# Gated-recurrence trunk on one core: the first heads' pk in a free buffer, lb behind the last values, and the 64-row level beside the block product

## The chip, the core and the metric

One core of one Trainium2 chip runs the whole program. The metric is device microseconds (us) for one execution, the median of several runs. Each run's time lies a little above the span that its profile shows, which counts from the first to the last instruction.

## The reference

Two layers, each on 256 rows of 1024 columns (float32):

```
h = rmsnorm(x); proj = h @ w_in            # split into hq hf hi hg aq ak av ga gb
f  = lb + (1-lb)*sigmoid(hf); k = 1-f; q = silu(hq); v = hi     # 8 heads of 128
S_t = f_t * S_(t-1) + k_t v_t^T ;  o_t = q_t S_t                # gated linear recurrence
y_a = (rmsnorm_per_head(o) * silu(hg)) @ w_pa
y_b = sliding_window_attention(aq, ak, av, sinks) @ w_pb        # 16 query, 4 key heads of 64
x  += (sigmoid(ga)*y_a + sigmoid(gb)*y_b) @ w_o
x  += (silu(h2 @ w_gate) * (h2 @ w_up)) @ w_down                # h2 = rmsnorm(x)
```

and a last rmsnorm. The recurrence is written out as scores: score(t, s) is the sum over the 128 columns c of q(t,c) k(s,c) times the product of f(c) over the rows after s up to t.

## The kernel before

**The main stream.** All large products (the projections, yb, ya, wo, the feed-forward) are run by TensorE as matmuls of 128 x 128 by 512 columns. Every weight is split into a high and a low part (wh by ScalarE, wl by VectorE) ahead of its use, and each product takes three matmuls (wh by high, wl by high, wh by low). A generator of the main stream gives way after every 6 such matmuls; this is called a step here. In the order of the main stream a layer runs akv, aq, v, then pb (the forget gate and query of the recurrence), gate, gb and yb in halves, ga, ya, wo, and then the feed-forward. gate, gb, yb and ga have 48 matmuls in each half.

**Side work.** Attention, recurrence, norms and transposes are generators on a list; after each step of the main stream every one whose count of steps has run out is moved on. So the matmuls of side work stand between those of the main stream in groups, called visits here. The numbers that such a generator yields (`YB`, `YD`, `YQ`, `YN`, `GAPS`) are how many steps to let pass: they set where a visit stands. Instructions of the other engines are put in order by a scheduler, engine by engine; TensorE's in visits are kept as written. A helper records every operation, so that nearly all instructions of a trace have its line, L57, and go by the names of their tiles.

**Attention** (`attention`): for four groups n of heads, `attend` makes scores (qk), `turn` transposes the weights (pt; ScalarE copies them back into the tile sp), and `values` multiplies them with v (pv). The tile sp is one buffer with the tag "sp". After `turn(3)`, `YB` steps pass, and then the last two `values` run in one visit.

**Recurrence** (`recurrence`, `decays`, `chain`): heads go in two halves, g = 0 and g = 1, and each has a `chain`. `decays` makes f, q and k. The chain makes the scores within 128 rows level by level, from 4 rows up: pk (VectorE products of q with f) and lb for blocks of 4; p2 and lc for blocks of 16; lv for the levels of 16, 32 and 64 rows; each time VectorE multiplies f into q and k for the next level, and the scores are gathered in sd and st. lx is the block product between rows 0 to 127 and 128 to 255, o the product with v (sx is the copy of lx that it reads), ot the transpose of the normed result, which ya reads. One visit serves both halves, with g = 1 one phase behind: the visits of a layer are lb of g = 0 alone, then lb with lc, lc with lv of 16 rows, lv 16 with lv 32, lv 32 with lv 64, lv 64 with lx, lx with o, o with ot, and ot alone. lb and lc write 32 rows of the output at a time, as do lv of 16 and 32 rows (the trace's forms 128\*32); lv of 64 rows and pv write 64 (128\*64); lx, o, ot, pt and the main stream write all 128 (128\*128).

**What the change touches.** The tile pk of g = 0, and p2 after it, lie in the buffer of the tag "sp", which is attention's until its last `values` are done; those of g = 1 lie in the buffer "pk", which is free. `recurrence` waits until attention has ended (`while atd[0] is not None`) before it starts the chain of g = 0, whose first part makes pk. The lv of 64 rows multiplies q and k in place for lx after its matmuls were issued, so lx can only stand one visit later. Small tiles with the tag "hx" share four buffers.

## Time and profile before

| | |
|---|---|
| median of 3 runs | 936.68 us (935.9 to 936.97) |
| the profiled execution | 936.02 us, span 934.3 us |
| instructions | 14356 |
| TensorE matmul busy | 923.8 us, 99% of the span |
| VectorE busy | 674.9 us, 72% |
| ScalarE busy | 536.8 us, 57% |
| mean granted TensorE clock | 0.999 |

The table's busy times are of the whole span. An engine's idle time is listed with what ended it, and an instruction's row in order of time gives its start, its length, its engine, what it wrote and read, and its shape (contraction rows \* output rows, then the moving tile). A float32 product counts as two matmuls in a trace, one of the main stream as one. Matmul ends are modelled and overlap the next start, so for TensorE only the distances between starts are used.

### The profile page before, as it was taken

How to read it: one execution, taken by the hardware profiler on the slowest of the kernel's cores; microseconds unless marked ns; L12 is line 12 of the kernel's file. 1: busy time of each engine (PE TensorE's matmuls, PEld its weight loads, DVE VectorE, ACT ScalarE, POOL GpSimd, SP SyncE). 2: the span in 40 equal slices, each digit the busy share in tenths (PEclk: the TensorE clock that was granted, in tenths of full speed). 3: DMA queues.
4: the chain of work that ended last, by engine and by line, in shares of the span. 5: the costliest groups of instructions: out<-in, count | busy, mean ns of one | idle time of the engine just before them, and what ended most of it. 6: DMA issues, size and time to landing. Idle time of an engine off the chain costs nothing.

```text
span 934.3 us, 14356 instructions
## 1 busy us (share of the span) xinstructions
PE 923.8 (99%) x5716; PEld 779.7 (83%) x5716; DVE 674.9 (72%) x1169; ACT 536.8 (57%) x906; POOL 21.1 (2%) x33
## 2 busy tenths in 40 slices
PE   8999999999999999999999999999999999999997
PEld 6878888888888888888888888888888888888885
DVE  5667679974778767766756677799667787667665
ACT  5665795465546555554555767945454565455553
POOL 2000000001000000000000000000010000000000
PEclk9999999999999999999999999999999999999999
DMA  7846435554545665566477444545545465556641
GB/s 277 236 150 212 136 98 167 191 178 135 172 144 184 195 202 186 181 190 203 164 157 238 135 136 140 176 151 179 169 155 183 158 201 183 181 184 204 195 139 46
DMA packets 111459, 161.40 MB, mean 173 GB/s; under 512 B 2976, under 2 KB 64736, under 8 KB 111392
## 3 DMA queue, kind: packets, MB, share of 16 engines
q1 hardware_dynamic: 110608, 159.38, 53.3%
q8 instruction: 45, 0.74, 0.3%
q10 hardware_dynamic: 560, 0.84, 0.3%
q0 software_dynamic: 224, 0.26, 0.1%
q14 instruction: 22, 0.18, 0.1%
HBM read 159.42 MB, written 1.05 MB: 172 GB/s over the span
## 4 chain that ended last, share of the span: by engine, by line
PE 89%; ACT 5%; DVE 4%; issue 0%; POOL 0%; DVEq 0%; ACTq 0%; POOLq 0%
PE pg L57 13%; PE pu L57 13%; PE acc L57 13%; PE pb L57 7%; PE gb L57 5%; PE ga L57 5%; PE v L57 5%; PE yb L57 5%; PE wo L57 5%; PE ya L57 5%; PE aq L57 5%; PE akv L57 2%; DVE wl L57 2%; ACT sp L57 1%; ACT wh L57 1%; PE o L57 1%
## 5 line engine op out<-in xcount | busy, mean ns | idle before, releaser
L57 DVE TENSOR_TENSOR wl<-raw,wh 128x1024 fp32r<-128x1024 f32 (+1 forms) x301 | 364.5, 1219 | 136.7 <-ACT wh L57 135.5
L57 ACT CAST wh<-raw 128x1024 fp32r<-128x1024 f32 (+1 forms) x301 | 314.0, 1049 | 171.8 <-PE acc L57 47.7
L57 PE MATMUL pu<-xx_n,wh 128*128 128x512 f32 x352 | 92.6, 393 | 0.0
L57 PE MATMUL pg<-xx_n,wh 128*128 128x512 f32 x352 | 92.1, 393 | 0.0
L57 PEld LDWEIGHTS pg<-xx_n,wh 128*128 128x128 f32 x352 | 63.2, 189 | 11.0
L57 PEld LDWEIGHTS pu<-xx_n,wh 128*128 128x128 f32 x352 | 63.1, 189 | 10.9
L57 PE MATMUL acc<-wh,ah 128*128 128x512 f32 x174 | 68.2, 392 | 0.0
L57 PE MATMUL acc<-wh,al 128*128 128x512 f32 x174 | 67.8, 391 | 0.0
L57 PE MATMUL acc<-wl,ah 128*128 128x512 f32 x174 | 67.8, 390 | 0.0
L57 PE MATMUL pb<-xx_n,wh 128*128 128x512 f32 x256 | 66.3, 396 | 0.0
L57 PEld LDWEIGHTS pb<-xx_n,wh 128*128 128x128 f32 x256 | 45.4, 189 | 8.9 <-DVE wl L57 0.7
L57 PEld LDWEIGHTS pg<-xx_n,wl 128*128 128x128 f32 x352 | 48.4, 190 | 4.1 <-ACT xx_n L57 0.6
L57 PEld LDWEIGHTS pu<-xx_n,wl 128*128 128x128 f32 x352 | 48.4, 190 | 3.6
L57 PE MATMUL pg<-xx_n,wl 128*128 128x256 f32 x352 | 50.3, 284 | 0.0
L57 PE MATMUL pu<-xx_n,wl 128*128 128x256 f32 x352 | 49.8, 283 | 0.0
L57 ACT COPY zg<-pg 128x256 f32<-128x256 f32 x44 | 16.4, 372 | 53.4 <-PE pg L57 53.4
L57 PE MATMUL ga<-wh,xx_n 128*128 128x512 f32 x128 | 41.5, 396 | 0.0
L57 PE MATMUL gb<-wh,xx_n 128*128 128x512 f32 x128 | 41.2, 393 | 0.0
L57 ACT ACTIVATE sp<-sp,stat 128x128 f32<-128x128 f32 (+1 forms) x64 | 28.2, 442 | 22.5 <-DVE stat L57 22.5
L57 PE MATMUL gate<-wh,xx_n 128*128 128x512 f32 x128 | 41.0, 394 | 0.0
L57 PE MATMUL v<-wh,xx_n 128*128 128x512 f32 x128 | 41.0, 394 | 0.0
L57 PE MATMUL aq<-wh,xx_n 128*128 128x512 f32 x128 | 40.3, 391 | 0.0
(240 smaller groups left out, 1662.9 us busy)
## 6 DMA issues: line engine op xcount, KB each, us to landing
raw<-in_w_in SPq DMA_DIRECT2D x58, 1024.0 KB, 5.3
raw<-in_w_gate SPq DMA_DIRECT2D x22, 1024.0 KB, 5.0
raw<-in_w_up SPq DMA_DIRECT2D x22, 1024.0 KB, 5.1
raw<-in_w_down SPq DMA_DIRECT2D x22, 1024.0 KB, 5.0
raw<-in_w_pb SPq DMA_DIRECT2D x8, 1024.0 KB, 5.0
raw<-in_w_pa SPq DMA_DIRECT2D x8, 1024.0 KB, 5.1
raw<-in_w_o SPq DMA_DIRECT2D x8, 1024.0 KB, 4.9
raw<-in_w_in SPq DMA_DIRECT2D x3, 512.0 KB, 6.2
```

What stands on the lines that cost most here:

```text
L57: ins = call(*args, **kw)
```

## The change

Three things are edited, and the two tables of steps with them.

1. The tags of pk and p2 are exchanged: g = 0 takes the buffer "pk", g = 1 the buffer "sp".
2. The chain of g = 0 is started (its pk made) before `recurrence` waits for attention's end, and attention's generator ends right with its last `values` (no `yield 3` behind it). The lb of g = 0 is issued in the same pass of the side work, straight behind the pv of the last values. The last values themselves stand 5 steps behind `turn(3)` and not 3.
3. The level of 32 rows now also writes the operands of lx into two new tiles, qx and kx ("hx"): two halves are multiplied by VectorE into them (before: in place), two are copied by ScalarE. So lv of 64 rows and lx of the same half stand in one visit, and a chain has one phase less. `GAPS` has 8 entries and not 9.

```
-YB, YD, YQ = 3, 2, 5
+YD, YE, YQ = 2, 5, 5
-GAPS = ((8,), (6, 7), (3, 5), (3, 3), (2, 3), (1, 2), (3, 2), (4, 2), (1,))
+GAPS = ((8,), (6, 7), (3, 5), (4, 3), (3, 3), (4, 2), (4, 4), (1,))
...
             turn(3)
-            yield YB
+            yield YE
             together(values(2, "at"), values(3, "at"))
-            yield 3
...
-            pk = sm.tile([P, 32, 80], F32, tag=("sp", "pk")[g], name=f"pk{l}{g}", bufs=1)
+            pk = sm.tile([P, 32, 80], F32, tag=("pk", "sp")[g], name=f"pk{l}{g}", bufs=1)
...
-            p2 = sm.tile([P, 64, 24], F32, tag=("sp", "pk")[g], name=f"p2{l}{g}", bufs=1)
+            p2 = sm.tile([P, 64, 24], F32, tag=("pk", "sp")[g], name=f"p2{l}{g}", bufs=1)
...
-            m = 16
-            while m <= 64:
+            for m in (16, 32):
...
-                elif m == 64:
-                    A.copy(st[0:64, :, 64:128], ps[0:64])
...
-                    V.tensor_tensor(q4[:, :, 3], q4[:, :, 3], f4[:, :, 2, 0:1].to_broadcast([P, 4, m]), ALU.mult)
-                    V.tensor_tensor(k4[:, :, 0], k4[:, :, 0], f4[:, :, 1, 0:1].to_broadcast([P, 4, m]), ALU.mult)
...
+                    qx, kx = (ztile([P, 4, P], f"{n}x{l}{g}", "hx") for n in "qk")
...
+                    A.copy(qx[:, :, 0:64], q4[:, :, 2])
+                    A.copy(kx[:, :, 64:P], k4[:, :, 1])
+                    V.tensor_tensor(qx[:, :, 64:P], q4[:, :, 3], f4[:, :, 2, 0:1].to_broadcast([P, 4, 64]), ALU.mult)
+                    V.tensor_tensor(kx[:, :, 0:64], k4[:, :, 0], f4[:, :, 1, 0:1].to_broadcast([P, 4, 64]), ALU.mult)
                 yield
-            ps = psum(f"lx{l}{g}", tag).rearrange("p (i c) -> p i c", c=P)
+            ps = psum(f"lv{l}{g}64", tag).rearrange("p (i c) -> p i c", i=8)
+            for i in range(8):
+                h, a = i // 2, i % 2 * P
+                T.matmul(ps[0:64, i, :], k[:, h, a:a + 64], q[:, h, a + 64:a + P], start=True, stop=True)
+            px = psum(f"lx{l}{g}", tag).rearrange("p (i c) -> p i c", c=P)
             for h in range(4):
-                T.matmul(ps[:, h, :], k[:, h, 0:P], q[:, h, P:S], start=True, stop=True)
+                T.matmul(px[:, h, :], kx[:, h, :], qx[:, h, :], start=True, stop=True)
             yield
             sx = ztile([P, 4, P], f"sx{l}{g}", "hx")
-            A.copy(sx, ps)
+            A.copy(st[0:64, :, 64:128], ps[0:64])
+            A.copy(sx, px)
...
             yield YD
+            chains = [chain(g) for g in range(2)]
+            next(chains[0])
+            yield 1
             while atd[0] is not None:
                 yield 1
-            chains = [chain(g) for g in range(2)]
-            next(chains[0])
-            yield 2
```

In the programs' order the first number after a tile's name is the layer and the second the half g (lb000 is layer 0, g = 0, its first part); numbers behind an underscore are buffers. The first place is TensorE's queue in layer 0 at the first lb. Before, it stands between matmuls of gate:

```order
L57 MATMUL gate10_1_1455<-wh42_1406,xx_n1_0_123 128x512
L57 MATMUL gate10_0_1454<-wh42_1406,xx_n1_0_123 128x512
L57 MATMUL lb000_1502<-pk00_1479,k00_178 32x80 x16
L57 MATMUL lb001_1519<-pk00_1479,k00_178 32x80 x16
L57 MATMUL gate10_0_1454<-wl42_1407,xx_n1_0_123 128x512
```

In the changed program, the same place in TensorE's queue:

```order
L57 MATMUL pv03_1465<-sp0_505,akv00_151 64x256
L57 MATMUL pv03_1465<-sp0_505,akv01_152 64x128
L57 MATMUL lb000_1478<-pk00_1365,k00_178 32x80 x16
L57 MATMUL lb001_1495<-pk00_1365,k00_178 32x80 x16
L57 MATMUL gate10_0_1438<-wh41_1378,xx_n1_0_123 128x512
```

lb moved behind the last pv: the visit with both stands 30 matmuls behind turn(3)'s pt, where before pv stood 18 and lb 49 behind it. The lb with lc follows 48 matmuls after that (before 47 after lb).

The second place is VectorE's queue in layer 0, at the products that make pk of g = 0. Before, they stand behind the last att0l, which reads what pv wrote:

```order
L57 TENSOR_TENSOR att0l1_167<-pv03_1437,att0h1_166 128x2x256
L57 TENSOR_TENSOR wl44_1469<-raw22_1370,wh44_1468 128x1024
L57 TENSOR_TENSOR pk00_1479<-pk00_1479,f00_176 128x32x24
L57 TENSOR_TENSOR wl45_1493<-raw22_1370,wh45_1492 128x1024
L57 TENSOR_TENSOR pk00_1479<-pk00_1479,f00_176 128x32x16
L57 TENSOR_TENSOR q00_177<-pk00_1479,f00_176 128x256
L57 TENSOR_TENSOR pk00_1479<-pk00_1479,f00_176 128x32x8
```

In the changed program, VectorE's queue at pk of g = 0:

```order
L57 TENSOR_SCALAR f01_179<-f01_179 128x1024
L57 TENSOR_TENSOR pk00_1365<-pk00_1365,f00_176 128x32x24
L57 TENSOR_TENSOR q00_177<-pk00_1365,f00_176 128x256
L57 TENSOR_TENSOR pk00_1365<-pk00_1365,f00_176 128x32x16
L57 TENSOR_TENSOR wl41_1379<-raw20_1266,wh41_1378 128x1024
L57 TENSOR_TENSOR pk00_1365<-pk00_1365,f00_176 128x32x8
```

The three products moved from behind wl44 to ahead of wl42, right behind the forget gates; on ScalarE's queue the copy that pk starts from likewise stands right behind the last k, ahead of wh41 and the copies into sp.

The third place is TensorE's queue in layer 0 at the lv of 64 rows of g = 1. Before:

```order
L57 MATMUL ga00_1_2158<-wh62_2102,xx_n1_0_123 128x512
L57 MATMUL lv0164_2208<-q01_180,k01_181 64x64 x8
L57 MATMUL lx00_2217<-q00_177,k00_178 128x128 x4
L57 MATMUL ga00_0_2157<-wh62_2102,xx_n1_0_123 128x512
L57 MATMUL ga00_0_2157<-wl62_2103,xx_n1_0_123 128x512
```

In the changed program, the same place in TensorE's queue:

```order
L57 MATMUL ga00_1_2169<-wh61_2092,xx_n1_0_123 128x512
L57 MATMUL lv0164_2219<-q01_180,k01_181 64x64 x8
L57 MATMUL lx01_2228<-qx01_2185,kx01_2186 128x128 x4
L57 MATMUL o000_2233<-v00_158,st_60 128x128 x4
L57 MATMUL o001_2238<-v00_158,sx00_2143 128x128
```

lx of g = 1 moved forward by a visit to its own lv, and o of g = 0 follows in the same visit; likewise lx of g = 0 now stands behind the lv of 64 rows of g = 0. From the visit of lv 16 with lv 32 on, 42, 36, 36 and 48 matmuls of the main stream stand between visits (before 36, 30, 18, 30 and 36). A layer has 8 visits from the last pv on, where before it had 10.

## The prediction

> **What bounds the kernel now.** I read the page first: its busy times and its chain of work that ended last.

> ```profile
> span 934.3 us, 14356 instructions
> PE 923.8 (99%) x5716; PEld 779.7 (83%) x5716; DVE 674.9 (72%) x1169; ACT 536.8 (57%) x906; POOL 21.1 (2%) x33
> PE 89%; ACT 5%; DVE 4%; issue 0%; POOL 0%; DVEq 0%; ACTq 0%; POOLq 0%
> ```

> TensorE is the bound: 99% busy, 89% of the chain. The kernel gets faster only by what leaves TensorE's queue: matmuls, waits, or time lost in going from one kind of matmul to another. The change removes no matmul. So I asked for TensorE's waits, and then for the chain in order of time, for the pace of the main stream:

> ```profile
> PE lb L57 <- DVE pk L57: 1.0, 2, 0.5
> 167.33 10.88 PE yb L57 x48
> ```

> TensorE waits for pk once in each layer, about 0.5 us each time: two waits, 1.0 us. That is the one wait that a visit of the recurrence has. The second row gives the price of one matmul of 512 columns: 10.88 / 48 = 0.227 us. Against this pace the cost of any visit can be read from the starts around it. TensorE in order of time around the last pv and the first lb of layer 0:

> ```profile
> 137.97 0.39 PE L57 MATMUL gate<-wh,xx_n 128*128 128x512 f32 x1
> 138.29 2.87 PE L57 MATMUL pv<-sp,akv 128*64 128x256 f32 x32
> 141.09 0.50 PE L57 MATMUL gate<-wh,xx_n 128*128 128x512 f32 x1
> ...
> 147.80 0.61 PE L57 MATMUL gate<-wh,xx_n 128*128 128x512 f32 x2
> 148.91 1.31 PE L57 MATMUL lb<-pk,k 128*32 128x80 f32 x64 [0.49 <-DVE pk L57]
> 150.15 0.50 PE L57 MATMUL gate<-wl,xx_n 128*128 128x512 f32 x1
> 150.49 0.62 PE L57 MATMUL gate<-wh,xx_n 128*128 128x512 f32 x2
> 150.95 0.40 PE L57 MATMUL gate<-wl,xx_n 128*128 128x512 f32 x1
> ```

> From 147.80 to 150.95 are 3.15 us. Five matmuls of gate start in that time and are worth 5 x 0.227 = 1.13, so the visit of lb costs 2.02 us, of which 0.49 is the wait.

> **Part 1: lb goes behind the last pv.** What does lb cost inside a visit, where nothing is switched? The later visit of lb with lc tells:

> ```profile
> 160.71 0.39 PE L57 MATMUL gb<-wh,xx_n 128*128 128x512 f32 x1
> 161.03 1.31 PE L57 MATMUL lb<-pk,k 128*32 128x80 f32 x64
> 162.16 0.86 PE L57 MATMUL lc<-p,k 128*32 128x48 f32 x64
> 162.96 0.50 PE L57 MATMUL gb<-wh,xx_n 128*128 128x512 f32 x1
> 163.29 0.40 PE L57 MATMUL gb<-wl,xx_n 128*128 128x512 f32 x1
> ```

> lb to lc takes 162.16 - 161.03 = 1.13 us, both being of form 128\*32. Entering costs 161.03 - 160.71 - 0.227 = 0.09. After the visit the first matmul of gb takes 0.33 and not 0.227, another 0.10. So lb's visit of 2.02 is 1.13 of work, 0.49 of wait and 0.40 of entering, leaving and starting again after the wait. In the merged visit lb pays 1.13 and one junction J, from form 128\*64 (pv) to 128\*32 (lb); the merged visit's entering and leaving were already paid by pv. The gain is 2.02 - 1.13 - J = 0.89 - J in each layer.

> J does not occur in the trace of before. Its lower end is 0, what lb to lc costs (same form). Its upper end is 0.32, a whole leaving and entering: the 2.02 without wait and work would then fall by 0.08 only. The nearest rows are the reverse junction, from 128\*32 to 128\*64, in the levels:

> ```profile
> 180.86 0.89 PE L57 MATMUL lc<-p,k 128*32 128x48 f32 x64
> 181.56 0.77 PE L57 MATMUL lv<-q,k 128*32 128x32 f32 x64
> 182.26 0.50 PE L57 MATMUL gb<-wh,xx_n 128*128 128x512 f32 x1
> 193.37 1.25 PE L57 MATMUL lv<-q,k 128*32 128x32 f32 x96
> 194.56 0.50 PE L57 MATMUL yb<-wh,att0h 128*128 128x512 f32 x1
> 202.94 1.77 PE L57 MATMUL lv<-q,k 128*32 128x32 f32 x48
> 204.64 0.50 PE L57 MATMUL ga<-wh,xx_n 128*128 128x512 f32 x1
> 211.67 1.15 PE L57 MATMUL lv<-q,k 128*64 128x64 f32 x16
> 212.74 1.16 PE L57 MATMUL lx<-q,k 128*128 128x128 f32 x8
> 213.66 0.48 PE L57 MATMUL ga<-wh,xx_n 128*128 128x512 f32 x1
> 217.62 0.39 PE L57 MATMUL ga<-wh,xx_n 128*128 128x512 f32 x1
> 217.85 1.05 PE L57 MATMUL lx<-q,k 128*128 128x128 f32 x8
> ```

> lc takes 181.56 - 180.86 = 0.70, and in the visit before it 162.96 - 162.16 = 0.80 with its end: leaving takes 0.10 there. Then the level of 16 is 0.70 - 0.10 = 0.60 for 64 matmuls, that of 32 is 1.19 - 0.60 - 0.10 = 0.49 for 32, and the level of 64 with its end 212.74 - 211.67 = 1.07. The visit of 32 with 64 takes 204.64 - 202.94 = 1.70, so 1.70 - 0.49 - 1.07 = 0.14 is the junction. I take J = 0.14: it is also a change of form inside a visit, and between the same two forms. Gain of part 1: 0.75 in a layer, 1.50 in both.

> [...] No row shows 64 to 32.

> **Part 2: lx beside lv of 64 rows.** No gain worth speaking of. Entering lx from the main stream takes 217.85 - 217.62 = 0.23, the plain pace, since both have form 128\*128. The visit that disappears is of that form, and costs nothing but its work. Changes of form in these visits are the same before and after: stream to 32 to 64 to stream, stream to 64 to lx; afterwards stream to 32 to 64 to lx, stream to 64 to lx. One leaving in a layer now ends in lx and not in the stream; the first lx behind lv may be a little cheaper or dearer than the first matmul of the stream, and I allow 0 to 0.05 us and take 0.02, an estimate.

> The moved work has other engines' price. In each layer ScalarE gets four copies of 128 x 256, and the four products of VectorE only change where they write. The nearest copy is

> ```profile
> L57 ACT COPY zg<-pg 128x256 f32<-128x256 f32 x44 | 16.4, 372 | 53.4 <-PE pg L57 53.4
> L57 DVE TENSOR_TENSOR wl<-raw,wh 128x1024 fp32r<-128x1024 f32 (+1 forms) x301 | 364.5, 1219 | 136.7 <-ACT wh L57 135.5
> ```

> so 4 x 0.37 = 1.5 us of ScalarE in a layer, and ScalarE is busy for 57% of the span (the second row is the price of a weight on VectorE, 1.2, used below). I cost it at nothing: between the visits involved now stand 42 and 36 matmuls (9.5 and 8.2 us), and what has to be done between them on ScalarE is four evacuations and copies of 0.4 to 0.6. Without that cover each copy would cost its 0.37. The level of 64, lx, o and ot get more room than before nearly everywhere (36 matmuls ahead of o, where before were 18).

> **What is late next.** The products that make pk, and the copy ahead of them, now stand ahead of weights and of sp:

> ```profile
> 134.51 1.16 ACT L57 ACTIVATE k<-f,ones 128x1024 f32<-128x1024 f32 x1
> 136.50 1.54 ACT L57 COPY sp<-pt 128x512 f32<-128x512 f32 x3
> 142.87 2.01 ACT L57 COPY pk<-q 128x1024 f32<-128x1024 f32 x2
> 135.78 0.69 DVE L57 TENSOR_SCALAR f<-f 128x1024 f32<-128x1024 f32 x1
> 144.94 0.95 DVE L57 TENSOR_TENSOR pk<-pk,f 128x768 f32<-128x768 f32 x1
> 151.23 0.48 DVE L57 TENSOR_TENSOR sd<-lb,cf 128x128 f32<-128x128 f32 x2
> 157.81 0.42 DVE L57 TENSOR_TENSOR p<-p,f 128x256 f32<-128x256 f32 x1
> ```

> The copy into pk (1.0) runs from 135.7, and delays the copies into sp from 138.0 to 139.1. The pv that read them stand 12 matmuls later, at 138.29 + 2.72 = 141.0: 1.9 us of cover. VectorE starts pk at 136.7; the first product takes 0.95, and with the two shorter ones (0.95 each at most), one product into q (0.6) and one weight (1.2) it is done by 141.4. lb is due at 141.0 + 2.8 = 143.8: 2.4 us of cover or more. So the wait of 0.49 goes whole; it came of pk being made only after pv had given up sp.

> The tightest place is then the visit of lb (g = 1) with lc. TensorE resumes at about 145.1 and comes to it 48 matmuls later, at 156.0. VectorE, between lb and p2, needed 151.23 to 158.23, or 7.0, with one weight of 1.2 among it. In the new order no weight stands there, but two products into q and the first of pk of g = 1 do: 0.95 for the latter, and 0.6 each for the former (128 x 256; p's of that size takes 0.42, a pass over 128 x 1024 0.69). That is 7.0 - 1.2 + 2.1 = 7.9. It starts after att0l, at 146 to 147, and ends at 154 to 155. Cover is 1 to 2 us for pk of g = 1, and one more for p2.

> **Sum.** Against the profiled execution: 934.3 - 1.50 - 0.04 = 932.8 of span, 936.02 - 1.5 = 934.5 of time. The median of the runs shown is 936.68, or 0.66 above the profiled execution; from it, 935.1. With J at its ends the gain is 1.1 to 1.9. About 0.2% (1.87 us) is what a measurement of this kernel can tell from no change, so the forecast lies just below that line.

> **The rivals.**

> *The junction is free, and the removed wide visit is worth something.* J = 0 and 0.05 for each part 2 gives 2 x (0.89 + 0.05) = 1.9, and about 2.0 if entering behind pv also saves lb's slow first matmuls: 934.7. For it: between lb and lc nothing is lost. Against it: the 0.14 between 32 and 64.

> *The wait is only moved.* If sp or pk is late in the merged visit by as much as lb waits now (cover of 1.9 and 2.4 us used up), 0.49 in each layer stays, and the gain is 0.5: 936.2. ScalarE's queue is the one to do it: copy, weight and sp stand in a row there.

> *Slower: lb with lc waits for VectorE.* Its place is the one with 1 to 2 us of cover. Each us by which pk of g = 1 is late beyond that costs 2 us in the program. To eat the gain and 0.2% more it must wait (1.5 + 1.9) / 2 = 1.7 us in each layer, so VectorE must be some 3 us later than worked out, about three weights of 1.2 in its way: 938.6. In the new order they stand behind p2, which speaks against it.

> **How the numbers follow.** The forecast, 935.1 with 934.7 to 935.7, gets 0.57; the free junction 0.28; the moved wait 0.10; slower 0.05. Since forecast and free junction lie at both sides of the line of 0.2%, and medians of before scatter by 1 us, some of each falls on the other side: faster 0.35, same 0.59, slower 0.06. The range 934.1 to 936.4 holds the first two cases and the moved wait, with that scatter.

> **What would show it.** Right: the list of TensorE's waits has no row of pk; the merged visit takes 2.80 + 1.13 + 0.14 = 4.1 us from the first pv to the next gate; from the last pv to the next visit of lb with lc no bracket; the visit of lv 64 with lx and o begins with 0.32 from the stream, and its span is the sum of its parts. Wrong: a row of TensorE waiting for pk, p, sp or kx; a merged visit of 3.9 us (the junction is free) or of over 4.2 (it is dear); a weight (wl or wh) that ends a wait of TensorE in gate or gb.

## The result and the profile after

| | before | after |
|---|---|---|
| median of 20 runs each | 936.65 us (935.87 to 937.65) | 938.73 us (937.6 to 940.15) |
| the profiled execution | 936.02, span 934.3 | 937.85, span 936.1 |

The ratio is 1.0024, with an interval of 1.0018 to 1.0030: slower by 2.1 us. The prediction said 935.1, with 934.1 to 936.4 as its range, and gave 0.06 to slower. The profiled execution after is one of the shorter of its 20, so the two profiles differ by 1.8 and not by 2.1.

The page of the kernel after: span, busy times, the chain by engine.

```profile
span 936.1 us, 14386 instructions
PE 923.7 (99%) x5716; PEld 779.3 (83%) x5716; DVE 673.8 (72%) x1169; ACT 539.1 (58%) x914; POOL 19.7 (2%) x33
PE 81%; DVE 11%; ACT 5%; issue 2%; DMA 2%; DVEq 0%; ACTq 0%
```

TensorE's work is what it was. But the chain, of which VectorE had 4%, now has 11% of it, and "issue" rose from 0 to 2%: TensorE waits at places where it did not. The list of TensorE's waits in the kernel after (us in total, times, longest):

```profile
PE gb L57 <- issue: 2.0, 1, 2.0
...
PE lc L57 <- DVE p L57: 0.7, 2, 0.4
```

The row of pk is gone, as forecast, and two new rows stand there: lc waits for p in each layer, and one matmul of gb waits 2.0 us for nothing that a semaphore tells ("issue"). The merged visit after, TensorE in order of time:

```profile
140.79 0.39 PE L57 MATMUL gate<-wh,xx_n 128*128 128x512 f32 x1
141.11 2.87 PE L57 MATMUL pv<-sp,akv 128*64 128x256 f32 x32
143.91 1.31 PE L57 MATMUL lb<-pk,k 128*32 128x80 f32 x64
145.16 0.50 PE L57 MATMUL gate<-wh,xx_n 128*128 128x512 f32 x1
```

No row has a bracket (the mark of a wait), and 145.16 - 141.11 = 4.05 us: the part that was worked out went as forecast. The next visit, lb with lc, costs 2.15 as before and does not wait. The one after it, lc of g = 1 with lv of 16 rows, in the kernel after:

```profile
175.79 0.39 PE L57 MATMUL yb<-wh,att0l 128*128 128x512 f32 x1
176.56 0.88 PE L57 MATMUL lc<-p,k 128*32 128x48 f32 x63 [0.38 <-DVE p L57]
...
177.96 0.50 PE L57 MATMUL yb<-wh,att0h 128*128 128x512 f32 x1
...
179.47 0.39 PE L57 MATMUL gb<-wh,xx_n 128*128 128x512 f32 x1
181.88 0.39 PE L57 MATMUL gb<-wl,xx_n 128*128 128x512 f32 x1 [2.02 <-issue]
```

Entering it takes 176.56 - 175.79 - 0.227 = 0.54, where before it took 0.09; and six matmuls of yb and one of gb behind the visit TensorE stands still. In layer 1 the wait on p is nearly the same (0.41) and the standstill is absent. From costs of the visits in both traces (distance of the matmuls around a visit, less 0.227 for each):

| | us in the program |
|---|---|
| pv and lb in one visit, 4.28 for 3.03 + 2.03, twice | -1.56 |
| lx beside lv of 64 rows, 7.68 for 7.71, twice | -0.06 |
| lc waits for p, 0.45 twice | +0.90 |
| standstill behind lc, layer 0 | +2.19 |
| sum | +1.47 |

The spans differ by 1.8; of the rest, 0.25 is lost at one matmul of acc near the end of the program, and what is left is not assigned.

### The profile page after: what moved, and what is told of

It reads as the page before. It is cut to its first block, busy times and chain, and to the rows that moved or that the text cites. A ratio compares the mean times of both kernels' runs of the same rounds, so it can differ in the third digit from the quotient of the medians.

```text
span 936.1 us, 14386 instructions
## 1 busy us (share of the span) xinstructions
PE 923.7 (99%) x5716; PEld 779.3 (83%) x5716; DVE 673.8 (72%) x1169; ACT 539.1 (58%) x914; POOL 19.7 (2%) x33
## 3 DMA queue, kind: packets, MB, share of 16 engines
q1 hardware_dynamic: 110608, 159.38, 53.4%
HBM read 159.42 MB, written 1.05 MB: 171 GB/s over the span
## 4 chain that ended last, share of the span: by engine, by line
PE 81%; DVE 11%; ACT 5%; issue 2%; DMA 2%; DVEq 0%; ACTq 0%
PE pg L57 13%; PE pu L57 13%; PE acc L57 12%; PE pb L57 7%; PE v L57 5%; PE wo L57 5%; PE ya L57 5%; PE aq L57 5%; PE ga L57 5%; DVE wl L57 4%; PE yb L57 3%; PE gb L57 2%; PE akv L57 2%; DVE q L57 2%; ACT wh L57 1%
## 5 line engine op out<-in xcount | busy, mean ns | idle before, releaser
L57 DVE TENSOR_TENSOR wl<-raw,wh 128x1024 fp32r<-128x1024 f32 (+1 forms) x301 | 363.9, 1218 | 133.7 <-ACT wh L57 131.6
L57 ACT CAST wh<-raw 128x1024 fp32r<-128x1024 f32 (+1 forms) x301 | 313.2, 1049 | 176.6 <-PE acc L57 47.7
L57 PE MATMUL pu<-xx_n,wh 128*128 128x512 f32 x352 | 92.6, 393 | 0.0
L57 PE MATMUL pg<-xx_n,wh 128*128 128x512 f32 x352 | 92.0, 392 | 0.0
L57 PEld LDWEIGHTS pg<-xx_n,wh 128*128 128x128 f32 x352 | 63.1, 189 | 11.0
L57 PEld LDWEIGHTS pu<-xx_n,wh 128*128 128x128 f32 x352 | 63.0, 189 | 11.0
L57 PE MATMUL acc<-wh,ah 128*128 128x512 f32 x174 | 68.2, 392 | 0.1
L57 PE MATMUL acc<-wh,al 128*128 128x512 f32 x174 | 67.7, 390 | 0.0
L57 PE MATMUL acc<-wl,ah 128*128 128x512 f32 x174 | 67.7, 389 | 0.0
L57 PE MATMUL pb<-xx_n,wh 128*128 128x512 f32 x256 | 66.3, 395 | 0.0
L57 PEld LDWEIGHTS pb<-xx_n,wh 128*128 128x128 f32 x256 | 45.4, 189 | 8.9 <-issue 0.7
L57 PEld LDWEIGHTS pg<-xx_n,wl 128*128 128x128 f32 x352 | 48.4, 190 | 4.1 <-ACT xx_n L57 0.6
L57 PEld LDWEIGHTS pu<-xx_n,wl 128*128 128x128 f32 x352 | 48.4, 190 | 3.6
L57 PE MATMUL pg<-xx_n,wl 128*128 128x256 f32 x352 | 50.3, 284 | 0.0
L57 PE MATMUL pu<-xx_n,wl 128*128 128x256 f32 x352 | 49.7, 282 | 0.0
L57 ACT COPY zg<-pg 128x256 f32<-128x256 f32 x44 | 16.4, 373 | 53.3 <-PE pg L57 53.3
L57 PE MATMUL gb<-wh,xx_n 128*128 128x512 f32 x128 | 41.2, 393 | 0.0
L57 ACT ACTIVATE sp<-sp,stat 128x128 f32<-128x128 f32 (+1 forms) x64 | 28.2, 442 | 22.5 <-DVE stat L57 22.5
L57 PE MATMUL gate<-wh,xx_n 128*128 128x512 f32 x128 | 40.9, 393 | 0.0
L57 PE MATMUL v<-wh,xx_n 128*128 128x512 f32 x128 | 40.9, 393 | 0.0
L57 PE MATMUL ga<-wh,xx_n 128*128 128x512 f32 x128 | 40.8, 392 | 0.0
L57 PE MATMUL aq<-wh,xx_n 128*128 128x512 f32 x128 | 40.3, 391 | 0.0
```

What stands on the lines that cost most here:

```text
L57: ins = call(*args, **kw)
```

## Why p is late

The visit of lc moved forward by 18 matmuls and by part 1's gain, 18 x 0.227 + 0.75 = 4.83 us: from 180.86 to 176.03, had it not waited. VectorE's products into p did not move as far. The last of them before:

```profile
178.61 0.42 DVE L57 TENSOR_TENSOR p<-p,f 128x256 f32<-128x256 f32 x1
```

and after, with the two that stand ahead of it:

```profile
175.06 0.68 DVE L57 TENSOR_TENSOR p<-p,f 128x512 f32<-128x512 f32 x1
175.66 0.42 DVE L57 TENSOR_TENSOR q<-q,f 128x256 f32<-128x256 f32 x1
176.00 0.41 DVE L57 TENSOR_TENSOR p<-p,f 128x256 f32<-128x256 f32 x1
```

p was done at 179.03 and is now at 176.41: 2.62 earlier, where TensorE is 4.83 earlier. The cover before was 180.86 - 179.03 = 1.83, and 4.83 - 2.62 - 1.83 = 0.38 is the bracket. VectorE had no idle time in which to come earlier; only another order, with its weights (wl) behind p, could have done that, and this was not tried. Its busy time in windows of the kernel before (a row gives the window, its length, and the busy times of TensorE's matmuls, its weight loads, VectorE, ScalarE and GpSimd):

```profile
142.00:162.00 20.00, 19.51 (x196) 15.83 (x198) 20.00 (x35) 11.21 (x13) 0.00 (x0) 1.00 0.41 127
162.00:186.00 24.00, 24.00 (x307) 19.95 (x298) 23.93 (x47) 9.37 (x10) 0.00 (x0) 1.00 0.59 209
```

43.93 of 44 us: over the span VectorE is busy for 72%, in this stretch for all of it, and in the kernel after the same.

## What the standstill is

The trace has one more kind of transfer, the loading of instructions. The DMA queues on the page of the kernel after:

```profile
q8 instruction: 45, 0.74, 0.3%
```

45 packets with 0.74 MB, 16.4 KB each (every one has 16384 bytes). TensorE has 2 x 5716 = 11432 matmuls and weight loads; shared out over the 45 pieces, that is 254 to a piece. The packets come one at a time, all along the program: the first starts when TensorE has begun 187 instructions, the last at 11417, so 44 steps of 255.2 in the mean, in the kernel before as in the one after (median 252.5 and 254, single steps 27 to 409). The expectations below take a piece at 256. That this queue carries TensorE's code is inferred from these counts. So the theory (A) was, as the author's assumption and not as something that a trace shows: TensorE's sequencer, the part that reads its instructions, runs some way ahead of the array that does the work, and when it enters a piece, the load of the next one starts; but at an instruction that waits for a semaphore it is held. lc's visit (with lv of 16 rows) is 256 instructions that run in 1.4 us (176.56 to 177.96), less than the 2.4 us from the start of a load to TensorE's going on (below). If the sequencer is held by p at lc just ahead of a border between pieces, the load starts only when p is done, and TensorE has run through its whole piece before it lands. DMA queues of the kernel after, first from 162 to 177 us, then from 176.4 to 181.9:

```profile
q1 hardware_dynamic: 1352, 2.67, 54.7%
...
q1 hardware_dynamic: 534, 1.06, 58.7%
q8 instruction: 1, 0.02, 1.1%
```

and of the kernel before, from 165 to 180 us (its lc comes at 180.86):

```profile
q8 instruction: 1, 0.02, 0.4%
```

Before, a piece is loaded ahead of lc; after, none is in the 15 us up to lc, and one starts at 179.47, 3.1 us after p. TensorE goes on 2.4 us after that start. The rival (B) was that gb's weight or another engine's lateness ends the standstill, and the code's place has nothing to do with it. In what follows a place is a count of TensorE's instructions in the trace up to that point (matmuls, weight loads, and 16 to 18 of the sequencer's own); lc of g = 1 in layer 0 is at place 2261 before and 2227 after, and the standstill is at 2497.

The 3.1 us between p and the load have a cause of their own. What the DMA queues moved in the kernel after, in GB/s: two windows ahead of p, then the stretch from 176.4 to 181.9 us in 40 slices:

```profile
174.00:175.00 1.00, 1.00 (x6) 0.84 (x5) 1.00 (x2) 0.09 (x1) 0.00 (x0) 1.00 0.00 0
175.00:176.00 1.00, 1.00 (x6) 0.64 (x4) 1.00 (x3) 0.96 (x1) 0.00 (x0) 1.00 0.00 0
...
GB/s 104 60 89 89 134 149 164 402 372 447 402 402 402 432 402 387 432 402 402 417 432 402 387 179 30 0 0 0 0 0 0 0 0 0 30 45 45 60 45 89
```

Ahead of p the queues moved nothing (the last figure of the first two rows). The kernel before and experiments 3 and 6 below start this load when TensorE is at place 2200; the kernel after is there at 173.07, and yet its load does not start in these idle 2 us: something held the request, and p at lc is what TensorE waits for there. Which part of TensorE is held, the sequencer or a queue behind it, the traces do not show. From 177.4 to 179.6 a weight of 1 MB takes the queues, and the load starts as that transfer ends. It does so in every trace with a standstill (in all five within 0.3 us of the transfer's end), and in each profile here 24 to 33 of the 45 loads start within 0.5 us of such an end, where about 7 would by chance. So the request came late by p, and then stood behind a weight. An estimate from these rows: a load that had started at p's end, 176.41, would have been in use 2.4 us later, at 178.8, ahead of the place 2497, due at 179.7. By that it took both to stop TensorE; no run varied the weight.

No run shows how many pieces TensorE has at hand at a time. That the border lies a piece of 256 places ahead of the standstill (2497 - 256 = 2241) is the author's estimate; by the count above a piece is 255.2.

## Experiments

**1 and 2: shift the code, ahead of the place and behind it.** The first kernel writes 16 products of layer 0's first lb a second time, for 8 columns alone, the second kernel 16 of lv of 16 rows (g = 1), a visit behind lc; both have 64 instructions more. (The code is abridged here.)

```
+ if l == g == half == 0:                  # first
+     T.matmul(ps[32*j:32*j+32, i, 0:8], k[:, h, ts_], pk[:, 8*h+4*t+j, 0:8], ...)
+ if l == 0 and g == 1 and i < 4:          # second
+     T.matmul(ps[32*j:32*j+32, i, 0:8], k[:, h, ts_], q[:, h, a+32*j:a+32*j+8], ...)
```

> The changed kernel with 16 small products more in layer 0, in the first visit of lb (g = 0): each repeats a product of lb on 8 of its 80 columns and writes the same values. This moves TensorE's later instructions on by 64. Theory A (code loading): the wait of 2.0 us behind the visit of lc with lv 16 is TensorE out of instructions. They come in pieces of 16 KB, 256 instructions, and the visit, which was held for p, begins just ahead of the end of a piece. Moved on by 64 the border is passed before the visit is held: that wait goes, the 0.4 us for p in each layer stays, and the small products cost about 0.4. 936.9 us, 1.8 less than the changed kernel. Theory B (a late weight or another result behind the visit, since VectorE is behind): the wait stays, about 939.1.

> Control for the run before: the same number of small products, but in the visit of lv 16 (g = 1) with lv 32 of layer 0, one visit behind the wait of 2.0 us. Theory A: nothing ahead of the wait has moved, so it stays at 2.0 us, and the time is that of the changed kernel and some 0.4 for the products, about 939.1. If more small products in a program removed the wait wherever they stand, 936.9.

Measured: 935.75 with the shift ahead (ratio to before 0.9996, 0.9986 to 1.0005) and 938.26 with it behind (1.0024, 1.0015 to 1.0033). TensorE's waits with the shift ahead:

```profile
...
PE lc L57 <- DVE p L57: 0.4, 1, 0.4
```

and with it behind:

```profile
PE gb L57 <- issue: 1.9, 1, 1.9
...
PE lc L57 <- DVE p L57: 0.8, 2, 0.4
```

The same added work takes the standstill away when it stands ahead of lc, and leaves it when it stands behind. It is the place in the code that counts: B falls. The first is 1.1 us better than A said. About half of that is the level of that set of runs: beside them the kernel before took 936.13 and not 936.65. Another part is p's wait in layer 0, which fell from 0.45 to 0.21 since the added products make lc 0.3 later.

**3: lc 18 matmuls later**, at place 2263, where it stood before the change.

```
-GAPS = ((8,), (6, 7), (3, 5), (4, 3), (3, 3), (4, 2), (4, 4), (1,))
+GAPS = ((8,), (6, 10), (3, 5), (3, 3), (3, 3), (4, 2), (3, 4), (1,))
```

> The changed kernel with the visit of lc (g = 1) with lv 16 three steps later (18 matmuls, 4.1 us; GAPS (6, 10) for (6, 7)), and two later gaps shorter by one. Theory A: p is ready 3.7 us ahead of the visit, so TensorE does not wait for it (0.9 less in both layers), its sequencer is not held there, and the border of the piece comes ahead of the visit (36 instructions more stand before it): the 2.0 go too. What is left is the gain of the merged visit: about 935.1, or 1.6 below before. If only the wait for p goes and that of 2.0 stays (theory B: something else is late there): 937.3.

Measured: 934.58 (934.3 to 935.4), ratio 0.9984 (0.9975 to 0.9994), the fastest of all. All of TensorE's waits:

```profile
PE warm L57 <- POOL ident L57: 1.6, 1, 1.6
PE akv L57 <- ACT xx_n L57: 1.2, 2, 0.9
```

With that visit put back both waits are gone, and the span of 932.9 is 1.4 below before: the 1.62 of parts 1 and 2 in the table above, less the 0.25 of acc, which is here too.

**4: the old kernel with lc 12 matmuls earlier**, at place 2237, and nothing of the change.

```
-GAPS = ((8,), (6, 7), (3, 5), (3, 3), (2, 3), (1, 2), (3, 2), (4, 2), (1,))
+GAPS = ((8,), (6, 5), (3, 7), (3, 3), (2, 3), (1, 2), (3, 2), (4, 2), (1,))
```

> The kernel before, with one edit: its visit of lc (g = 1) with lv 16 two steps earlier (12 matmuls, 2.7 us; GAPS (6, 5) and (3, 7) for (6, 7) and (3, 5)). None of the change is in it. p was ready 1.8 us ahead of this visit. Theory A and VectorE's lateness: TensorE waits about 0.9 us for p in each layer, and the visit now begins 24 instructions nearer to the last border, with the next border just inside it while the sequencer is held: a wait of about 2 us follows in layer 0. About 936.65 + 1.8 + 2 = 940.4, or 938.5 if the border is missed. If the waits belong to the change (its buffers, its copies on ScalarE, its order of weights): within 0.5 of before, 936.7.

Measured: 939.72, ratio 1.0038 (1.0023 to 1.0052). Its waits:

```profile
PE lc L57 <- DVE p L57: 1.9, 2, 1.0
...
PE gb L57 <- issue: 1.1, 1, 1.1
PE lb L57 <- DVE pk L57: 1.0, 2, 0.5
```

Both new waits appear without the change, by an earlier lc alone. Here the standstill comes two matmuls of gb behind the visit, and not seven matmuls, but at the same place, 2497.

**5 and 6: each part alone.** The first has part 1's edits on the old kernel; the second is the changed kernel with part 1's edits and the order up to lc of g = 1 undone. Shown is the line of the steps alone.

```
 first, against before           second, against after (tags of pk and p2, start of the chain: likewise)
-YB, YD, YQ = 3, 2, 5           -YD, YE, YQ = 2, 5, 5
+YD, YE, YQ = 2, 5, 5           +YB, YD, YQ = 3, 2, 5
```

> The old kernel with part 1 alone (lb behind the last pv, first heads' pk in the free tile); the level of 64 rows and the products of the blocks keep their own visits. lc of the second heads stands at the same 1104th matmul as in the changed kernel. Theory A (part 1 moved that visit 4.8 us forward, into VectorE's late p and ahead of a border of TensorE's code): both waits are here too, the list of waits has gb <- issue of about 2.0 and lc <- p of about 0.7, and the time is that of the changed kernel, 938.7 (2.0 above before). Theory B (part 2, by its four copies on ScalarE in each layer and its masks, is what delays VectorE's p): no wait on p, no stall, 935.1 as predicted for part 1.

> The changed kernel without part 1: lb in a visit of its own with the tile that pv gives up, all up to lc of the second heads in the old order (that visit at the 1122nd matmul), then the level of 64 rows with lx. Theory A: the wait on pk is back (1.0 in the list), no wait on p and no stall, time of before within 0.2%: 936.6 (935.9 to 937.4). Theory B (part 2 is what costs): 938.2 or more.

Measured: part 1 alone 939.18, ratio 1.0026 (1.0016 to 1.0037); part 2 alone 936.44, ratio 1.0002 (0.9992 to 1.0011). TensorE's waits with part 1 alone, then with part 2 alone:

```profile
PE gb L57 <- issue: 2.3, 1, 2.3
PE lc L57 <- DVE p L57: 0.8, 2, 0.4
...
PE lb L57 <- DVE pk L57: 1.0, 2, 0.5
```

Part 1 alone has the standstill at place 2497 and the waits on p; part 2 alone has neither, and pk's wait is back. The loss came with part 1, by where it put lc.

**7 and 8: how sharp is the border?** The edit of the first experiment, for 4 and for 8 products of the 16.

```
+ if l == g == half == i == 0:             # 4 products
+ if l == g == half == 0 and i < 2:        # 8 products
```

> The changed kernel with 4 small products written twice in layer 0's first lb, so that TensorE's code behind it stands 8 instructions later. lc of the second heads is at the 2235th place of TensorE's stream, the border at the 2241st by the place where the three stalled runs stopped, 256 earlier. Theory A (TensorE's sequencer, held at lc by p, reaches the border only when p is done, and the load of the piece behind the next border starts only then): lc is still ahead of the border, the stall of about 2.0 stays, 938.6. Theory B (the pad of 64 instructions took the stall away by spreading the dense visit, in proportion to its length): an eighth of the 2.0 goes, also 938.5; the next kernel tells.

> The same with 8 products written twice: 16 instructions, lc of the second heads at the 2243rd place, two behind the border. Theory A: the sequencer passes the border long before it is held at lc; the load is early, the stall is gone whole, the wait on p of 0.3 to 0.4 stays in each layer, 936.3 (2.3 below the kernel with 4). Theory B: a quarter of the stall goes, 938.2.

These texts count two instructions for a product; it is four, since a float32 product is two matmuls and two weight loads in the trace (lb's 32 products are 64 matmuls and 64 loads). So lc is at place 2243 with 4 products and at 2259 with 8. Measured: 941.81 with 4 (ratio 1.0059, 1.0044 to 1.0074), 935.43 with 8 (0.9990, 0.9981 to 0.9999): four small products more make the kernel 6.4 us faster. Both theories had said about 938.5 for 4 products, and neither foresaw a longer standstill. TensorE with 4 products:

```profile
176.99 0.88 PE L57 MATMUL lc<-p,k 128*32 128x48 f32 x63 [0.32 <-DVE p L57]
...
177.70 0.74 PE L57 MATMUL lv<-q,k 128*32 128x32 f32 x62
182.32 0.21 PE L57 MATMUL lv<-q,k 128*32 128x32 f32 x1 [3.88 <-issue]
182.46 0.80 PE L57 MATMUL yb<-wh,att0h 128*128 128x512 f32 x1
183.05 0.63 PE L57 MATMUL yb<-wl,att0h 128*128 128x512 f32 x1
```

and with 8:

```profile
176.50 0.88 PE L57 MATMUL lc<-p,k 128*32 128x48 f32 x63 [0.28 <-DVE p L57]
...
177.21 0.76 PE L57 MATMUL lv<-q,k 128*32 128x32 f32 x63
177.90 0.50 PE L57 MATMUL yb<-wh,att0h 128*128 128x512 f32 x1
```

With 4, TensorE stops at place 2497 once more, which is now inside the visit: reached 1.4 us earlier than in the kernel after, while TensorE goes on 0.4 us later, so the standstill grows from 2.0 to 3.9. Its load again starts as the weight's transfer ends, at 180.13. With 8, lc still waits for p by 0.28, but nothing stops. All or nothing within 16 instructions is what A says and a dense visit that merely takes long would not. A's border was off: by the stop less 256 it was put at 2241, and a lc at 2243 was to be free of it; it lies between 2243 and 2259, 254 to 238 places ahead of the stop. Instructions that leave no record in the trace may be the difference.

**9: the place with p early.** A has a part that the others do not separate: that p holds the sequencer. Here lc comes late, as in experiment 3, and 24 instructions fewer stand ahead of it (of 8 warming products at the start 6 are left out).

```
-    spin(4)
+    spin(1)
```

(at both places where `spin` is called; `GAPS` as in experiment 3).

> The kernel with lc 18 matmuls later, and 6 of the 8 products that only warm TensorE at the start and ahead of the first stage left out; each product counts four instructions (two matmuls, two loads), so all code behind stands 24 instructions earlier. lc of the second heads is then at the 2239th place, among the places (2227, 2237, 2243) at which four kernels stalled, but p is done at about 176.3, 3.7 us ahead of lc, as in the kernel with lc later. Theory A (the load of the next piece starts when the sequencer, held at lc by p, is let go; it lands some 5.5 us later): let go at 176.3 it has the piece at about 182, just when TensorE gets there (lc due at 180.0, and 256 instructions on at 181.5): a stall of 0 to 0.5 us, 934.6 to 935.1. Rival C (the place alone decides: a dense visit across this border stalls, whatever p does): a stall of 2.0 to 3.9, 936.6 to 938.5. Fewer warming products may slow the first microseconds of TensorE; that is read apart, from the first 20 us of the trace.

Measured: 936.75, ratio 1.0002 (0.9992 to 1.0011). No row of "issue" and none of p stand in the list of waits. TensorE there:

```profile
182.25 0.89 PE L57 MATMUL lc<-p,k 128*32 128x48 f32 x64
182.95 0.77 PE L57 MATMUL lv<-q,k 128*32 128x32 f32 x64
183.65 0.51 PE L57 MATMUL gb<-wh,xx_n 128*128 128x512 f32 x1
183.99 0.40 PE L57 MATMUL gb<-wl,xx_n 128*128 128x512 f32 x1
```

The time alone fell into C's range and not into A's. But what it is slower than experiment 3 (2.0 us of span) is lost at the start: the first aq comes at 23.60 and there at 21.45, since with less warming the early matmuls run at half pace for longer (akv's are still 0.43 apart at 12.29; in experiment 3 they are 0.23 apart at 10.98 already). At place 2239, among places that stall (2227, 2237, 2243), nothing stalls, so the place alone does not decide: C falls. DMA queues from 164 to 181.5 us, then from 178.4 to 182.7, with what they moved in 40 slices of the latter:

```profile
q1 hardware_dynamic: 1781, 3.54, 57.8%
...
q1 hardware_dynamic: 515, 1.02, 63.7%
q8 instruction: 1, 0.02, 1.3%
GB/s 210 0 0 0 38 133 305 286 362 362 419 381 400 419 419 419 381 438 400 400 419 400 419 400 400 419 400 400 324 134 172 0 0 0 0 0 0 0 0 0
```

No piece in the 17 us up to 181.5 (in experiment 3, with lc 24 places further on, it starts at 172.91, 7.2 us ahead of lc); here it starts at 181.71, 3.2 us after p was done (178.48), lands at 182.59, and is in use by 183.99, when place 2497 is due. Here too it starts as a weight's transfer ends, so most of the 3.2 us is the weight's. That p held it before that rests in this run on 0.4 us alone: TensorE was at place 2200 at 177.85, and the queues were idle until 178.28. With p done 3.8 us ahead of lc the load just came in time.

## Why the prediction was wrong

**Right:** the merged visit (4.05 for 4.07 worked out), so that the junction between the forms of 64 and 32 rows comes to 0.12 for 0.14; the gain of part 1 (0.78 for 0.75 in a layer) and of part 2 (0.03 for 0.02); sp and pk in time; no wait where lb stands with lc, in spite of a cover of 1 to 2 us. Experiment 3 is that forecast without the rest: 934.6 where 935.1 was said, and 1.55 below the kernel before beside it (936.13) where 1.54 was said.

**Wrong:** the step "what is late next". It followed VectorE through the visits up to lb with lc, called that the tightest place and stopped one visit short. The row of the next stands in the prediction for another purpose (lc at 180.86), and p of g = 1 was not followed: 1.83 us of cover, for a visit that moved 4.83 forward with an engine that is busy for 43.93 of the 44 us from 142 to 186. The rival "slower" had the right mechanism, TensorE waiting for VectorE, at the wrong visit, and asked for 1.7 us in each layer; the wait was 0.45. The working for lb with lc moved VectorE's weights behind p2 and let them speak against a wait; but there they stand ahead of the next visit's p, and they leave VectorE no idle time.

**Not there at all:** the standstill of 2.2 us. It is what takes the time out of the range and turns its sign: experiments 1 and 8, in which lc still waits for p and nothing stands still, have ratios of 0.9996 and 0.9990, or 936.3 and 935.7 from 936.65. No term and no rival dealt with TensorE's own code, whose queue (45 packets) was on the page. The trace of before had part of what such a term needs: a load of 0.9 us for every 255.2 of TensorE's instructions, and in lc with lv a visit of 256 instructions in 1.4 us (180.86 to 182.26), which the change moves to another place in the code.

## What to carry to other kernels

When a change moves a visit forward, follow every visit behind it to the end of the stage, and for each compare how far TensorE moves with how far its operands can move; an engine's slack is read in a window of that stage, not from its share of the span. A short wait on an operand can cost many times its own length, as 0.4 us did here ahead of 256 instructions that run in 1.4 us, with 2.0 to 3.9 us behind it: no code was loaded while TensorE waited, and the load started only as a weight's transfer ended (in the kernel after 3.1 us after p was done). Look for "issue" brackets, count TensorE's instructions there, and see what the DMA queues carry just ahead. Where a kernel has such a place, a few instructions more or less ahead of it can move the time by more than the change under test (16 of them moved it by 6.4 us here), so a change's worth is measured at more than one alignment.

## What the runs showed of the hardware

```profile
178.50:182.30 3.80, 0.00 (x0) 0.00 (x0) 3.01 (x7) 0.00 (x0) 0.00 (x0) 0.97 0.55 179
182.30:185.40 3.10, 3.08 (x8) 2.36 (x8) 2.35 (x5) 0.00 (x0) 0.00 (x0) 0.50 0.87 326
185.60:190.00 4.40, 4.40 (x21) 3.61 (x20) 3.02 (x5) 3.48 (x6) 0.00 (x0) 1.00 0.00 0
```

For 3.1 us matmuls of 512 columns start 0.43 apart, and 1.4 us are lost on top. After the standstill of 2.0 us in the profile of the kernel after, the next matmuls start 0.23 apart, at a granted clock of 1.00; after that of 2.3 us in experiment 5 they start 0.43 apart from 182.28 to 185.68, with a granted clock of 0.50 from 183 to 185 (mean of that execution 0.996). The runs without a profile fall apart the same way: of the kernel after, 7 of 20 have a mean clock of 0.996 and take 939.31 to 940.15 us, the others 0.997 to 0.999 and 937.6 to 939.12. That fits some 3 us at half clock (0.0017 of the span): by this estimate the standstill of about 2 us was followed by half clock in some executions and not in others, which is part of why the median lies above the profiled execution.
